# The first token block's experts chosen in two parts of four heads, the first part during the query projection

## The chip, the cores and the metric

The kernel runs on one core of a Trainium2 chip. The metric is device time in microseconds (us), the median over runs. The core has a tensor engine (PE, with its weight loads as PEld), a vector engine (DVE), an activation engine (ACT), a fourth engine (POOL), which after the start only gathers rows by index, and SP, which issues all the other transfers. Each engine works through its own instructions in order, and waits where an instruction needs another engine or a transfer.

## The reference: what is computed

A decoder layer over 1024 tokens of width 1024, in float32:

```python
h   = layer_norm(x)
mix = token_mixer(h)            # stick-breaking attention + mLSTM, gated, projected
h   = layer_norm(ALPHA * h + mix)
ffn = peer_ffn(h)               # experts
ple = sigmoid(h @ w_ple_gate) * (p @ w_ple)
h   = layer_norm(ALPHA * h + ffn + ple)
```

The experts (`peer_ffn`): for each token and each of 8 heads two query halves are scored against 128 keys each, the 16 best of each half are kept, the 16 best of their 256 sums are taken, and these give 16 of 16384 experts. So each token has 8 x 16 = 128 experts. With u and v the two tables of 16384 rows, a token's output is the sum over its experts of gate * gelu(h . u[expert]) * v[expert].

## The kernel before

**Blocks.** The tokens are cut into 8 token blocks of 128 (`tb` 0 to 7), one token on each partition. These are worked in three blocks: (0, 1), (2, 3, 4) and (5, 6, 7). Each block passes through `project`, `attention`, `recurrent`, `mlstm`, `branch`, `keys`, `choose` and `embed`; the next block's `pre` and `project` are merged into the end of the one before.

**Two ways to the experts.** Token blocks 7, 3 and 4 (`DENSE`) are done densely: `spread` turns the choice into a table of gates in DRAM (`Gd`), and `dense` then multiplies the tokens with all 16384 experts on PE, in 128 groups, at the end of the kernel. Token blocks 0, 1, 2, 5 and 6 are done by rows: for each of the 128 slots POOL gathers a 4 KB row for every token (512 KB in all, L1116), first from u and then from v, and DVE works on it with one scalar_tensor_tensor (listed under L142, a helper's line). That makes 5 x 256 = 1280 gathers. Their order is fixed: all u rows of a token block come before its v rows, and the v rows of one token block alternate with the u rows of the next, if that one's experts are known.

**Buffers.** Gathered rows go into six buffers of the tag `vr` (`K` = 6). For block 0 the same six buffers also hold, split into two halves for extra precision (`Halves`), the activations `o.h1` that `keys` and `embed` multiply: four of the six. They come free when `embed`'s last matmul with them is done.

**Query projection and choice.** `keys` projects the queries in four units; each gives two heads. For every half head, `best` finds the 16 best keys (five DVE operations on 128 x 128: L818 to L822). In block 0 the scores of the second token block are put aside (`o.hold`) and `best` is run for it later, inside `choose`. `choose` then does, for all 8 heads of a token block at once: 50 candidate sums (`cv`), the 16 best of them head by head, the candidates' expert numbers (`ci`), a match of positions to numbers (`eq`, `idf`), and the indices as integers (`vidx`); after that the gates (`gt`). The weights of block 0 are split in two on ACT and DVE before PE uses them (DVE's part is L259).

**Order.** The program is written by Python generators that yield planned microseconds. `Merge` interleaves generators by planned time. A background stream (`Experts`) is stepped whenever the planned time of the main work passes its own; one step writes a u row and a v row where both are due. In `Experts.add` a token block enters the list only when two calls have come: one from `choose` (gates ready), one from `embed` (its base sum `based` stored). The written order is a priority: a scheduler at compile time orders each engine's instructions on a modelled timeline. DVE operations of `choose` go through `cvec`, a chain of depth 20 (`CD`), those of the rows through `evec`, a chain of depth 1.

Of the kernel before, what the change touches and what calls it, by code (L numbers as in the profile page):

```python
# [73 lines left out]
FAST = {0}  # L74
FASTQ = {0}
SLOTS = 5
W = 384


# [43 lines left out]
def body(ctx: ExitStack, tc: tile.TileContext, a, out):  # L123
# [763 lines left out]
    def choose(o, tbs):  # L887
        for tb in tbs:
            j = tb - o.tbs[0]
            V, I = o.VI[j]  # L890
# [5 lines left out]
            t4 = csel("top", (P, 4, P))  # L896
            fI = t4[:, 0:2, :].rearrange("p a (h k) -> p a h k", h=NH)
            ts = t4[:, 2, :].rearrange("p (h k) -> p h k", h=NH)
            fp = t4[:, 3, :].rearrange("p (h k) -> p h k", h=NH)
            cvec.tensor_copy(fI, I)  # L900
            cvec.tensor_scalar(fI[:, 0], fI[:, 0], 128.0, None, op0=OP.mult)
            cv = csel("cv", (P, NH, NC50))
            ci = csel("ci", (P, NH, NC50))
            def sums(dst, src, of, a0, a1, b0, b1):
                na, nb = a1 - a0, b1 - b0
                d = dst[:, :, of:of + na * nb]
                l, r = src[:, 0, :, a0:a1], src[:, 1, :, b0:b1]
                if na == 1:
                    l = l.to_broadcast([P, NH, nb])
                elif nb == 1:  # L910
                    r = r.to_broadcast([P, NH, na])
                else:
                    d = d.rearrange("p h (a b) -> p h a b", b=nb)
                    l = l[:, :, :, None].to_broadcast([P, NH, na, nb])
                    r = r[:, :, None, :].to_broadcast([P, NH, na, nb])
                cvec.tensor_tensor(d, l, r, op=OP.add)

            for of, a0, a1, nb in RANKS:
# [12 lines left out]
            cvec.tensor_copy(fp, pos)  # L931
            cvec.tensor_scalar(fp, fp, STEP, None, op0=OP.mult)
            idf = T([P, NH, 16], F32, "idf", 1)
# [4 lines left out]
            cvec.tensor_tensor(ci, ci, posn[:, None, :].to_broadcast([P, NH, NC50]), op=OP.add)  # L938
            yield 2.5
            for i, (_, n) in enumerate(CLASSES):  # L940
                k = slice(4 * i, 4 * i + 4)
                step = NH if n * 4 * NH <= D else NH // 2
                for h in range(0, NH, step):
                    h = slice(h, h + step)
                    shape = [P, step, 4, n]
                    eq = c4("eq")[:, :step * 4 * n].rearrange("p (h k n) -> p h k n", h=step, k=4)
                    cvec.tensor_tensor(eq, ci[:, h, None, :n].to_broadcast(shape),
                                       fp[:, h, k, None].to_broadcast(shape), op=OP.subtract)
                    cvec.tensor_reduce(idf[:, h, k], eq, axis=AX.X, op=OP.min, apply_absolute_value=True)
                    yield 2 * (step * 4 * n + 60) * 1.05e-3  # L950
            vidx = T([P, P], U32, "vidx", 5)
            x = cvec.tensor_copy(vidx, idf.rearrange("p h k -> p (h k)"))
            gt = T([P, NH, 16], F32, "gt", 5)
            cvec.tensor_tensor(gt, ts, ts[:, :, 0:1].to_broadcast([P, NH, 16]), op=OP.subtract)
            act.loose(gt, gt, AF.Exp)
            sm = T([P, NH], F32, "sm", 1)
            cvec.tensor_reduce(sm, gt, axis=AX.X, op=OP.add)
            cvec.reciprocal(sm, sm)
            cvec.tensor_tensor(gt, gt, sm[:, :, None].to_broadcast([P, NH, 16]), op=OP.mult)
            if tb in DENSE:  # L960
                yield from spread(tb, vidx, gt)
            else:
# [137 lines left out]
    class Experts:  # L1100
        def __init__(self):
# [1 line left out]
            self.e = self.v = None  # L1103
            self.fifo = []
            self.rate = 1.0
            self.half = []

        def add(self, tb):

            self.half.append(tb)  # L1110
            if self.half.count(tb) == 2:
                self.todo.append(tb)

        def row(self, idx, s, use):
            vr = T([P, D], F32, "vr", K)
# [14 lines left out]
        def first(self, tb):  # L1130
# [146 lines left out]
```

## Time and profile before

| what | value |
|---|---|
| median of 3 runs | 3270.45 us (3263.51 to 3273.95) |
| profiled execution, own time | 3266.96 us |
| its span, first to last instruction | 3265.2 us |
| mean granted PE clock | 0.947 of full |
| busy: PE, DVE, POOL, ACT | 2928.7, 2616.4, 1571.5, 1086.9 us |
| moved by DMA | 1035.20 MB |

The own time is the span with 1.8 us around it. A busy share is a mean over stages that are limited by different things, so each stage is read by itself. Times in the rows are counted from the span's start.

### The profile page before, as it was taken

How to read it: one execution, taken by the hardware profiler on the slowest of the kernel's cores; microseconds unless marked ns; L12 is line 12 of the kernel's file. 1: busy time of each engine (PE TensorE's matmuls, PEld its weight loads, DVE VectorE, ACT ScalarE, POOL GpSimd, SP SyncE). 2: the span in 40 equal slices, each digit the busy share in tenths (PEclk: the TensorE clock that was granted, in tenths of full speed). 3: DMA queues.
4: the chain of work that ended last, by engine and by line, in shares of the span. 5: the costliest groups of instructions: out<-in, count | busy, mean ns of one | idle time of the engine just before them, and what ended most of it. 6: DMA issues, size and time to landing. Idle time of an engine off the chain costs nothing.

```text
span 3265.2 us, 39000 instructions
## 1 busy us (share of the span) xinstructions
PE 2928.7 (90%) x12201; PEld 1994.7 (61%) x12201; DVE 2616.4 (80%) x5551; ACT 1086.9 (33%) x2574; POOL 1571.5 (48%) x1313
## 2 busy tenths in 40 slices
PE   7997999969899937999898986999999999999990
PEld 7886655645464535667655554666666666666660
DVE  5635898898799998988987999977666777777788
ACT  5626335421621458656414135111111111111110
POOL 0000065667633543576765353455554555554564
PEclk9998999979999968999999998999999999999995
DMA  6444698989989978898899899999999999999997
GB/s 220 131 143 144 230 365 310 379 304 374 382 289 314 343 290 314 298 373 304 298 380 346 305 338 322 358 365 349 349 354 358 348 355 343 352 353 332 367 327 275
DMA packets 341823, 1035.20 MB, mean 317 GB/s; under 512 B 38512, under 2 KB 95216, under 8 KB 341616
## 3 DMA queue, kind: packets, MB, share of 16 engines
q0 software_dynamic: 184320, 671.17, 56.7%
q1 hardware_dynamic: 157296, 361.55, 30.7%
q8 instruction: 96, 1.57, 0.2%
q14 instruction: 111, 0.91, 0.1%
HBM read 991.17 MB, written 41.42 MB: 316 GB/s over the span
## 4 chain that ended last, share of the span: by engine, by line
PE 66%; DVE 16%; issue 7%; ACT 7%; DMA 4%; POOL 1%; SPq 0%; DVEq 0%; POOLq 0%; ACTq 0%
PE g L282 14%; PE g L1047 13%; PE z L1047 7%; PE m L286 5%; PE m L284 5%; PE m L285 5%; DVE acc L142 3%; PE g L798 3%; ACT ohB L164 2%; DVE vr L142 2%; PE g L286 2%; PE g L284 2%; PE g L285 2%; PE m L622 1%; PE m L1032 1%
## 5 line engine op out<-in xcount | busy, mean ns | idle before, releaser
L1116 POOL DMA_INDIRECT vr<-in_u_dram,vidx x640 | 782.0, 1222 | 982.4 <-DVE V L142 383.6
L1116 POOL DMA_INDIRECT vr<-in_v_dram,vidx x640 | 785.9, 1228 | 683.4 <-DVE acc L142 289.4
L142 DVE SCALAR_TENSOR_TENSOR acc<-vr,w,acc 128x1024 f32<-128x1024 f32 x640 | 818.8, 1279 | 57.1 <-DMA vr<-in_v_dram,vidx 47.1
L142 DVE SCALAR_TENSOR_TENSOR vr<-vr,h1r 128x1024 f32<-128x1024 f32 x640 | 780.3, 1219 | 64.8 <-DMA vr<-in_u_dram,vidx 51.4
L164 ACT ACTIVATE hl<-wf 128x512 fp32r<-128x512 f32 x240 | 151.2, 631 | 909.9 <-PE m L285 779.0
L1047 PE MATMUL g<-wf,y 128*128 128x512 f32 x960 | 431.3, 592 | 0.0
L259 DVE TENSOR_TENSOR hl<-wf,hl 128x512 fp32r<-128x512 f32 x240 | 167.7, 699 | 285.9 <-ACT hl L164 247.5
L284 PE MATMUL m<-h1s,hl 128*128 128x384 f32 x960 | 370.3, 386 | 0.0
L282 PE MATMUL g<-hT,wf 128*128 128x384 f32 x1024 | 343.1, 491 | 3.2 <-DVE gs L865 3.2
L286 PE MATMUL m<-h1s,hl 128*128 128x384 f32 x960 | 322.9, 336 | 0.0
L285 PE MATMUL m<-h1s,hl 128*128 128x384 f32 x960 | 322.2, 336 | 0.0
L1047 PEld LDWEIGHTS g<-wf,y 128*128 128x128 f32 x960 | 180.3, 189 | 173.0 <-issue 172.1
L282 PEld LDWEIGHTS g<-hT,wf 128*128 128x128 f32 x1024 | 193.1, 192 | 137.4 <-issue 11.0
L1047 PE MATMUL z<-wf,y 128*128 128x512 f32 x480 | 225.5, 592 | 0.0
L285 PEld LDWEIGHTS m<-h1s,hl 128*128 128x128 f32 x960 | 180.6, 188 | 28.7 <-issue 28.7
L284 PEld LDWEIGHTS m<-h1s,hl 128*128 128x128 f32 x960 | 180.6, 188 | 28.7 <-issue 28.7
L286 PEld LDWEIGHTS m<-h1s,hl 128*128 128x128 f32 x960 | 180.3, 188 | 0.0
L1001 PE MATMUL z<-ohA,ohB 128*128 128x128 f32 x768 | 134.5, 319 | 42.6 <-DVE ohB L999 17.5
L282 PE MATMUL g<-h1T,wf 128*128 128x384 f32 x512 | 172.5, 492 | 0.0
L1047 PEld LDWEIGHTS z<-wf,y 128*128 128x128 f32 x480 | 91.2, 190 | 114.8 <-issue 114.8
L1001 PEld LDWEIGHTS z<-ohA,ohB 128*128 128x128 f32 x768 | 111.6, 212 | 68.0 <-ACT ohB L164 46.1
L259 DVE TENSOR_TENSOR wf<-wf 128x1024 fp32r<-128x1024 f32 x68 | 83.1, 1222 | 69.9 <-ACT wf L164 67.1
(350 smaller groups left out, 4725.5 us busy)
## 6 DMA issues: line engine op xcount, KB each, us to landing
wf<-in_uE_dram SPq DMA_DIRECT2D x128, 512.0 KB
wf<-in_v_dram SPq DMA_DIRECT2D x128, 512.0 KB
wf<-in_wmain_dram SPq DMA_DIRECT2D x84, 512.0 KB
wf<-in_wgate_dram SPq DMA_DIRECT2D x48, 512.0 KB
wf<-in_wq_dram SPq DMA_DIRECT2D x48, 512.0 KB
Gd<-stage SPq DMA_DIRECT2D x48, 512.0 KB
gp<-Gd SPq DMA_DIRECT2D x32, 768.0 KB
wf<-in_wout_dram SPq DMA_DIRECT2D x24, 512.0 KB
```

The lines of the kernel that those rows point to most:

```text
L142: x = getattr(vec, op)(*args, **kw)
L164: x = nc.scalar.activation(o, i, f, **kw)
L259: vec.tensor_tensor(lo, src, hi, op=OP.subtract)
L282: pe.matmul(o, l[0], r[0], start=first, stop=last)
L284: pe.matmul(o, l[0], r[0], start=first, stop=False)
L285: pe.matmul(o, l[0], r[1], start=False, stop=False)
L286: pe.matmul(o, l[1], r[0], start=False, stop=last)
L622: pe.matmul(pw[:, c], sp[:, c], nident, start=False, stop=True, skip_group_check=True)
L798: pe.matmul(acc, yT[k // 4][:, k % 4, n * P:(n + 1) * P], wo[u][k // 2][:, k % 2, :], start=k == 0, stop=k == 7)
L1001: pe.matmul(pg[:, k], B[:, k], A[:, k], start=True, stop=True)
L1047: pe.matmul(acc[d][c], y[:, d * P:(d + 1) * P], wv[:, c * 512:(c + 1) * 512], start=e == 0, stop=e == P - 1)
L1116: pool.indirect_dma_start(out=vr, out_offset=None, in_=use[0], in_offset=bass.IndirectOffsetOnAxis(ap=idx[:, s:s + 1], axis=0))
```

## The change

`choose` for one token block becomes a generator `pick` that takes a list of head ranges. For token block 0 it gets two ranges, heads 0 to 3 and heads 4 to 7 (`PARTS`). The first part is merged into the third unit of the query projection (the one with number 2), behind the second unit, which delivers the last of heads 0 to 3; the second part runs where `choose` ran. After a part, `vidx` holds 64 of the 128 slots, and `Experts.known` lets the rows of these slots be written; `first` waits in planned time for the rest. For block 0 the u rows no longer wait for `embed`; the v rows still do (`stored`). All other token blocks are chosen in one range, with the same operations as before, but `pick` yields head by head (1.3 each) where `choose` yielded 2.5 for four heads, so that its planned cost is larger. In block 0 the scratch tile `eq` comes from the tag `c6` and no longer from `c4`.

```diff
+PARTS = {1: (0, 4), 3: (4, 8)}
...
+        o.pick = pick(o, o.tbs[0], PARTS.values()) if o.hold else None
+
+        def part():
+            for c in o.pick:
+                if c is None:
+                    break
+                yield c
+
         for u in range(4):
-            yield from gemm(o.q["q"][u], r1, range(4), ev_q(u), False, w)
+            g = gemm(o.q["q"][u], r1, range(4), ev_q(u), False, w)
+            yield from Merge(g, part()) if o.hold and u - 1 in PARTS else g
...
+            if o.hold and j == 0:
+                yield from o.pick
+            else:
+                yield from (c for c in pick(o, tb, [(0, NH)]) if c is not None)
+
+    def pick(o, tb, parts):
...
+        for h0, h1 in parts:
+            n = h1 - h0
+            hs = slice(h0, h1)
...
-            yield 2.0
-            pos = T([P, NH, 16], U32, "pos", 1)
-            for h in range(NH):
+            yield 0.25 * n
+            for h in range(h0, h1):
                 c = cv[:, h, :]
                 cvec.max(ts[:, h, 0:8], c)
...
-                if h % 4 == 3:
-                    yield 2.5
...
+                yield 1.3
...
-            yield 2.5
-            for i, (_, n) in enumerate(CLASSES):
+            yield 0.3 * n
+            for i, (_, m) in enumerate(CLASSES):
                 k = slice(4 * i, 4 * i + 4)
-                step = NH if n * 4 * NH <= D else NH // 2
-                for h in range(0, NH, step):
+                step = n if m * 4 * n <= D else n // 2
+                for h in range(h0, h1, step):
...
-                    eq = c4("eq")[:, :step * 4 * n].rearrange("p (h k n) -> p h k n", h=step, k=4)
...
+                    eq = (c6("eq", (P, 4 * W)) if o.hold else c4("eq"))[:, :step * 4 * m].rearrange("p (h k n) -> p h k n", h=step, k=4)
...
+            cs = slice(h0 * 16, h1 * 16)
+            x = cvec.tensor_copy(vidx[:, cs], idf[:, hs].rearrange("p h k -> p (h k)"))
+            if tb not in DENSE:
                 chosen[tb] = vidx, gt
-                cvec.gate = x if o.hold and j == 0 else None
-                ex.add(tb)
-                yield 1.0
+                ex.known(tb, h1 * 16)
+            if h1 < NH:
+                yield None
...
-            self.half = []
+            self.n, self.stored = {}, set()
+
+        def known(self, tb, n):
+
+            if tb not in self.n:
+                self.todo.append(tb)
+            self.n[tb] = n
 
         def add(self, tb):
 
-            self.half.append(tb)
-            if self.half.count(tb) == 2:
-                self.todo.append(tb)
+            self.stored.add(tb)
...
             for s in range(P):
+                while s >= self.n[tb]:
+                    yield ROW_US
...
-            if self.e is None and self.todo and len(self.ready) < 1:
+            if self.e is None and self.todo and len(self.ready) < 1 and (
+                    self.todo[0] in BLOCKS[0] or self.todo[0] in self.stored):
                 self.e = self.first(self.todo.pop(0))
-            if self.v is None and self.ready:
+            if self.v is None and self.ready and self.ready[0][0] in self.stored:
                 self.v = self.second(*self.ready.pop(0))
```

## Rows read from the trace of the kernel before

**Rows 1.** The page's chain that ended last, shares by engine.
```profile
PE 66%; DVE 16%; issue 7%; ACT 7%; DMA 4%; POOL 1%; SPq 0%; DVEq 0%; POOLq 0%; ACTq 0%
```

**Rows 2.** Windows: length; busy PE, PEld, DVE, ACT, POOL (xinstructions); clock, DMA share, GB/s.
```profile
2054.00:3184.00 1130.00, 1130.00 (x4351) 778.29 (x4349) 827.20 (x1354) 198.03 (x361) 596.09 (x476) 1.00 0.97 352
3184.00:3244.00 60.00, 0.55 (x2) 0.00 (x0) 54.89 (x46) 0.00 (x0) 40.49 (x36) 0.53 0.92 337
```

**Rows 3.** Timeline of POOL: start, length, what; idle before and its releaser.
```profile
2035.06 1.17 POOL L1116 DMA_INDIRECT vr<-in_v_dram,vidx  x1 [0.66 <-DVE top L142]
2054.20 0.94 POOL L1116 DMA_INDIRECT vr<-in_u_dram,vidx  x1 [17.97 <-DVE top L142]
```

**Rows 4.** DVE, choice of token block 5: first and last operation, rows' share (window).
```profile
2001.28 0.28 DVE L142 CAST top<-I 128x256 f32<-128x256 uint16 x1
...
2053.72 0.22 DVE L142 CAST vidx<-idf 128x128 uint32<-128x128 f32 x1
...
2001.00:2054.00 53.00, 20.36 (x16) 0.81 0.89 290
```

**Rows 5.** The chain that ended last, around the dense stage's start.
```profile
2004.95 6.19 DMA Gd<-stage
...
2011.21 12.08 DMA gp<-Gd
```

**Rows 6.** Timeline of POOL at its first gathers, 385 to 403 us.
```profile
385.91 1.09 POOL L1116 DMA_INDIRECT vr<-in_u_dram,vidx  x1 [381.68 <-DVE V L142]
...
392.27 0.94 POOL L1116 DMA_INDIRECT vr<-in_u_dram,vidx  x1 [0.30 <-issue]
402.88 0.94 POOL L1116 DMA_INDIRECT vr<-in_u_dram,vidx  x1 [9.67 <-DVE I L142]
```

**Rows 7.** DVE ends the second unit; then tile vr, 330 to 460 us, first:last start.
```profile
322.13 0.29 DVE L822 FIND_INDEX8 I<-V,sc 128x8 uint16<-128x128 f32 x1
...
L1116 POOL DMA_INDIRECT vr<-in_u_dram,vidx x33: 932/960/2252, 385.9 to 459.0; - x33
...
L286 PE MATMUL g<-wf,vr x32: 388/392/398, 342.1 to 372.2; 128*128 128x512 f32 x32
...
L142 DVE SCALAR_TENSOR_TENSOR vr<-vr,h1r x28: 1177/1222/1230, 401.4 to 458.7; 128x1024 f32<-128x1024 f32 x28
```

**Rows 8.** Windows at the query projection's end: all engines; L259 alone; L142 alone.
```profile
322.00:355.50 33.50, 32.93 (x220) 28.86 (x219) 22.52 (x76) 14.96 (x33) 0.00 (x0) 1.00 0.51 171
355.50:385.00 29.50, 29.24 (x103) 19.11 (x102) 29.40 (x132) 9.73 (x11) 0.00 (x0) 1.00 0.71 236
...
322.00:355.50 33.50, 11.11 (x10) 1.00 0.51 171
...
355.50:385.00 29.50, 20.30 (x117) 1.00 0.71 236
```

**Rows 9.** Timeline of DVE: five small sums of the choice, one after another.
```profile
371.43 0.51 DVE L142 TENSOR_TENSOR ci<-top 128x32 f32<-128x32 f32 x5
```

**Rows 10.** Timeline of POOL and DVE behind the last matmul.
```profile
3187.28 10.53 DVE L142 SCALAR_TENSOR_TENSOR acc<-vr,w,acc 128x1024 f32<-128x1024 f32 x8
3189.15 1.54 POOL L1116 DMA_INDIRECT vr<-in_v_dram,vidx  x1 [1.18 <-DVE acc L142]
3190.99 1.01 POOL L1116 DMA_INDIRECT vr<-in_v_dram,vidx  x1 [0.30 <-issue]
3192.31 1.02 POOL L1116 DMA_INDIRECT vr<-in_v_dram,vidx  x1 [0.30 <-issue]
...
3198.41 1.28 DVE L142 SCALAR_TENSOR_TENSOR acc<-vr,w,acc 128x1024 f32<-128x1024 f32 x1 [0.61 <-DMA vr<-in_v_dram,vidx]
```

**Rows 11.** DVE's waits for gathered u rows, whole run: total us, times, longest.
```profile
DVE vr L142 <- DMA vr<-in_u_dram,vidx: 51.4, 62, 2.1
```

**Rows 12.** Windows over the second block's choice and spread.
```profile
1000.00:1200.00 200.00, 167.50 (x624) 104.37 (x623) 193.21 (x566) 84.42 (x228) 101.02 (x82) 0.91 0.93 339
1200.00:1400.00 200.00, 144.30 (x689) 101.59 (x690) 182.65 (x355) 122.20 (x332) 97.87 (x78) 0.88 0.82 289
```

More of the change, by code (lines that the diff above doesn't have):

```diff
@@ L889, in choose @@
             j = tb - o.tbs[0]
-            V, I = o.VI[j]
             if o.hold and j == 1:
@@ new lines, in pick @@
+    def pick(o, tb, parts):
+        j = tb - o.tbs[0]
+        V, I = o.VI[j]
+        t4 = csel("top", (P, 4, P))
+        fI = t4[:, 0:2, :].rearrange("p a (h k) -> p a h k", h=NH)
+        ts = t4[:, 2, :].rearrange("p (h k) -> p h k", h=NH)
+        fp = t4[:, 3, :].rearrange("p (h k) -> p h k", h=NH)
+        cv = csel("cv", (P, NH, NC50))
+        ci = csel("ci", (P, NH, NC50))
+        pos = T([P, NH, 16], U32, "pos", 1)
+        idf = T([P, NH, 16], F32, "idf", 1)
+        vidx = T([P, P], U32, "vidx", 5)
+        gt = T([P, NH, 16], F32, "gt", 5)
+        for h0, h1 in parts:
+            n = h1 - h0
+            hs = slice(h0, h1)
@@ L904, in sums @@
             def sums(dst, src, of, a0, a1, b0, b1):
                 na, nb = a1 - a0, b1 - b0
-                d = dst[:, :, of:of + na * nb]
-                l, r = src[:, 0, :, a0:a1], src[:, 1, :, b0:b1]
+                d = dst[:, hs, of:of + na * nb]
+                l, r = src[:, 0, hs, a0:a1], src[:, 1, hs, b0:b1]
                 if na == 1:
-                    l = l.to_broadcast([P, NH, nb])
+                    l = l.to_broadcast([P, n, nb])
                 elif nb == 1:
-                    r = r.to_broadcast([P, NH, na])
+                    r = r.to_broadcast([P, n, na])
@@ L912, in sums @@
                 else:
                     d = d.rearrange("p h (a b) -> p h a b", b=nb)
-                    l = l[:, :, :, None].to_broadcast([P, NH, na, nb])
-                    r = r[:, :, None, :].to_broadcast([P, NH, na, nb])
+                    l = l[:, :, :, None].to_broadcast([P, n, na, nb])
+                    r = r[:, :, None, :].to_broadcast([P, n, na, nb])
                 cvec.tensor_tensor(d, l, r, op=OP.add)
+            cvec.tensor_copy(fI[:, :, hs], I[:, :, hs])
+            cvec.tensor_scalar(fI[:, 0, hs], fI[:, 0, hs], 128.0, None, op0=OP.mult)
@@ L928, in choose @@
                 cvec.max_index(pos[:, h, 8:16], ts[:, h, 8:16], c)
-                if h % 4 == 3:
-                    yield 2.5
-            cvec.tensor_copy(fp, pos)
-            cvec.tensor_scalar(fp, fp, STEP, None, op0=OP.mult)
-            idf = T([P, NH, 16], F32, "idf", 1)
+                yield 1.3
+            cvec.tensor_copy(fp[:, hs], pos[:, hs])
+            cvec.tensor_scalar(fp[:, hs], fp[:, hs], STEP, None, op0=OP.mult)
             for blocks, _ in CLASSES:
@@ L936, in choose @@
                     sums(ci, fI, to, *ab)
-            cvec.tensor_tensor(ci, ci, posn[:, None, :].to_broadcast([P, NH, NC50]), op=OP.add)
-            yield 2.5
-            for i, (_, n) in enumerate(CLASSES):
+            cvec.tensor_tensor(ci[:, hs], ci[:, hs], posn[:, None, :].to_broadcast([P, n, NC50]), op=OP.add)
+            yield 0.3 * n
+            for i, (_, m) in enumerate(CLASSES):
                 k = slice(4 * i, 4 * i + 4)
-                step = NH if n * 4 * NH <= D else NH // 2
-                for h in range(0, NH, step):
+                step = n if m * 4 * n <= D else n // 2
+                for h in range(h0, h1, step):
@@ L944, in choose @@
                     h = slice(h, h + step)
-                    shape = [P, step, 4, n]
-                    eq = c4("eq")[:, :step * 4 * n].rearrange("p (h k n) -> p h k n", h=step, k=4)
-                    cvec.tensor_tensor(eq, ci[:, h, None, :n].to_broadcast(shape),
+                    shape = [P, step, 4, m]
+                    eq = (c6("eq", (P, 4 * W)) if o.hold else c4("eq"))[:, :step * 4 * m].rearrange("p (h k n) -> p h k n", h=step, k=4)
+                    cvec.tensor_tensor(eq, ci[:, h, None, :m].to_broadcast(shape),
@@ L948, in choose @@
                                        fp[:, h, k, None].to_broadcast(shape), op=OP.subtract)
                     cvec.tensor_reduce(idf[:, h, k], eq, axis=AX.X, op=OP.min, apply_absolute_value=True)
[L950 to L962, printed above, removed]
-                chosen[tb] = vidx, gt
-                cvec.gate = x if o.hold and j == 0 else None
-                ex.add(tb)
-                yield 1.0
+                    yield 2 * (step * 4 * m + 60) * 1.05e-3
@@ new lines, in pick @@
+            cs = slice(h0 * 16, h1 * 16)
+            x = cvec.tensor_copy(vidx[:, cs], idf[:, hs].rearrange("p h k -> p (h k)"))
+            if tb not in DENSE:
+                chosen[tb] = vidx, gt
+                ex.known(tb, h1 * 16)
+            if h1 < NH:
+                yield None
+        cvec.tensor_tensor(gt, ts, ts[:, :, 0:1].to_broadcast([P, NH, 16]), op=OP.subtract)
+        act.loose(gt, gt, AF.Exp)
+        sm = T([P, NH], F32, "sm", 1)
+        cvec.tensor_reduce(sm, gt, axis=AX.X, op=OP.add)
@@ L968, in spread @@
+        cvec.reciprocal(sm, sm)
+        cvec.tensor_tensor(gt, gt, sm[:, :, None].to_broadcast([P, NH, 16]), op=OP.mult)
+        if tb in DENSE:
+            yield from spread(tb, vidx, gt)
+        else:
+            cvec.gate = x if o.hold and j == 0 else None
+            yield 1.0
     def spread(tb, vidx, gt):
```

8 lines of the change are left out of this document (removed).

## The prediction

> **What bounds the kernel now.** I read the page's chain that ended last first. PE has two thirds of it [rows 1], but a share doesn't say what a gather that comes earlier is worth, so I went to the windows from the end backwards. From 2054 to 3184 us, the dense stage, PE is busy all of the time, the DMA engines 0.97 of it, and POOL issues 476 gathers, one per 2.374 us (1130 / 476). Then PE is done, and 36 gathers are left, which take 60 us, 1.667 us each [rows 2]; after them come 21 us of layer norms. 476 + 36 = 512 are the gathers of token blocks 5 and 6. So the end hangs on two moments: **t5**, at which the first of these 512 can go, and **D**, at which the dense stage ends. If t5 comes x later and D comes y later, (y - x) / 2.374 more rows are done by D and each saves 1.667: the end moves by 0.702 x + 0.298 y.
>
> What sets t5? The timeline of POOL shows the last gather of token block 2 at 2035.06, then 18 us in which POOL has nothing to gather, and the first of token block 5 at 2054.20 [rows 3]. That one waits for `vidx` of block 5, cast at 2053.72; its choice began at 2001.28 [rows 4]. So the row stream has already run dry there. Gathers that start earlier in block 0 don't end the kernel earlier by themselves: they lengthen this dry stretch. They help only as far as DVE, which multiplies the rows, is then free for block 5's choice: within it DVE spends 20.36 us on 16 rows of token block 2 [rows 4]. D is set elsewhere: by the end of `spread`, then a store of 6.19 us and a load of 12.08 us of the gate table [rows 5].
>
> **What the change moves.** Now the first gather goes at 385.91, and six can be in flight before a buffer comes back at 402.88 [rows 6]. The scores of heads 0 to 3 have been searched by 322.4 (322.13 + 0.29) [rows 7].
>
> The cost of the first part: the choice takes 20.30 us of DVE under L142 in 355.5 to 385 [rows 8]. Some 1 us of that are the gates, which stay whole; half of the rest is 9.65 us. Counting in the diff, 24 sums for `ci`, 7 for `cv` and 6 copies, scalings and additions are issued twice with half the heads, and `eq` with its reduction 8 times each where it was 6: 41 more instructions. The maxima and their indices go head by head already and don't multiply. Five small sums take 0.51 us [rows 9], so I take 0.08 us of fixed cost each: 3.3 us, half of it in the first part, which is then 11.3 us. DVE was idle for 33.5 - 22.52 = 11.0 us in 322 to 355.5 [rows 8]: it fits, with nothing to spare. With three weight splits of 1.11 us (11.11 / 10 [rows 8]) ahead of parts of it, the first 64 indices stand at 322.4 + 11.3 + 3.3 = 337 us. Bounds: 334 without the splits, 355.5 if the best-key searches of the last two units go first. I take 338, because the part is written before those searches.
>
> How many rows get ahead: four of the six row buffers hold the activations until `embed`'s last matmul with them, at 372.2 [rows 7]. So for 34 us two buffers circulate. Behind the last matmul the row of the first of the eight rows in a run frees a buffer for the gather at 3189.15; two gathers later, at 3192.31, goes the row that DVE then has to wait for, until 3198.41 [rows 10]: 6.1 us from issue to data. With 1.22 us on DVE and 0.3 us to hand over, a buffer is back after 7.6 us, so a row goes every 3.8 us: 9 rows by 372.2. Then six buffers, at the steady 2.374 us: 6 rows by 385.9. **15 rows ahead**; at least 8 (two, then six), at most 20 (48 us at 2.374).
>
> The Trainium skill, DMA: Bandwidth & Descriptors, "Anatomy of one DMA", gives about 2.0 us plus the bytes over 436 GB/s for a transfer of this kind, an estimate of 3.2 us for 512 KB. The row shows 6.1 us, beside other gathers. By the page a buffer would be back after 4.7 us, some 20 rows would get ahead, and the end would come 0.9 us earlier than in the sum below, which goes by the row.
>
> The Trainium skill, SBUF — State Buffer, "SBUF: two separate sides", speaks against the change: POOL cannot write a gather's descriptors while DVE runs certain two-port operations, and DVE will be full just where the early gathers go. The first 33 gathers went beside a full DVE, and POOL's spans for them are 0.96 us at the median and 2.25 us at the longest [rows 7]: the rule doesn't show in most of them. Were all as long as the longest, a buffer would be back after 8.9 us, one row fewer would get ahead, and the end would come 0.9 us later than in the sum.
>
> **The sum.** Each row done early takes 20.36 / 16 = 1.27 us of DVE out of block 5's choice [rows 4]; 15 rows take out 19.1 us. Bounds: nothing, if the choice is held by something else, and 20.36, since more rows than 16 don't lie in it. The early stage costs something: the 3.3 us of extra instructions, and whatever PE loses where DVE's weight splits come late. PE is busy 32.93 of 33.5 and 29.24 of 29.5 us there [rows 8], so its loss would not be won back. I take 3 us for both together, from 0 (DVE's own idle time hides it) to 10 (three weight splits of block 0's last ten lost behind rows). The store and load of the gate table, 18.3 us, lie beside gathers; with fewer of these I take 2 us off, from 0 to 4. The other moved or added pieces I cost at nothing: no transfer is added, and `h1r`'s one load, on SP, lies beside DMA engines that are busy 0.51 of the time [rows 8] (a load late by all of its 6 us would cost two rows); `eq` in another tag is the same work, if a tile of that tag is free (if not, the second part is late, and with it rows that have a buffer only after 372.2).
>
> So x = 3 - 19.1 = -16.1 and y = 3 - 2 = +1, and the end moves by 0.702 * -16.1 + 0.298 * 1 = -11.0 us. From the profiled execution's own 3266.96 that is 3256; the median of its runs is 3.5 us higher, 3270.45, so for a median I say **3257**.
>
> **The rivals.**
>
> *Fewer rows get round.* If the scheduler doesn't pass the two free buffers round before the other four come back, 8 rows get ahead: x = 3 - 10.2 = -7.2, y = 2, the end -4.5 us: 3262. Or the choice of block 5 doesn't move with the rows, since its order on DVE was set on a modelled timeline, and the dry 18 us [rows 3] simply grow: x = y = 3, 3270. For it: the gain must pass through one choice of 53 us in which DVE also waits for the gate table. Against: DVE's rows in that stretch are real work in its order.
>
> *Slower: early rows hold up DVE.* DVE works in order, and with two buffers a row's multiplication follows its gather closely. If DVE stands for the whole 6.1 us once for each of the 4.5 pairs, that is 27 us, the weight splits queue behind it, PE waits for the splits, and everything later moves by 27 + 3 = 30 us: the end by 0.702 * (30 - 19.1) + 0.298 * 28 = +16 us, 3283. It decides from a loss of 24 us on (24 - 13.9 = 10 us). Against: in the whole run DVE waited for u rows 62 times, 2.1 us at the longest [rows 11], and 4.5 such waits are 9.5 us. For: those rows had six buffers.
>
> *The finer steps in all token blocks.* The planned cost of a choice grows by 5.3 (10.4 for 5.0, 2.4 for 2.5). In the second block three choices and two `spread` follow one another; this places them up to 16 planned us later against `embed` and `project`. PE is idle there for 32.5 + 55.7 us while DVE is busy 193 and 183 of 200 [rows 12]. Either sign: 16 us later for all, with the gain of 11, is 3272; 16 us of PE's idle time won is 3241.
>
> **How the numbers follow.** Chances: my sum 0.42, fewer rows or a choice that stays 0.30, DVE held up 0.15, the finer steps 0.13 (0.04 faster, 0.03 same, 0.06 slower). About 0.3%, 10 us, is what a measurement of this kernel can tell from no change. Faster by more: 0.46; within: 0.33; slower: 0.21. The sum's own range, with its costs at their bounds, is 3252 to 3264. The range takes in the fewer rows (3262, 3270) and the held-up DVE but for its worst, and on the other side part of the finer steps: 3243 to 3282.
>
> **What the profile would show.** The first gather of u at about 338, and some 9 gathers by 372, in pairs. In 322 to 372 PE still busy for over 97%. The last v gather of token block 2 about 35 us earlier against the choice of block 5, fewer than 6 rows inside that choice, and its `vidx` near 2038. The stretch behind the last matmul shortened from 36 gathers to about 29. I am wrong if the first gather comes after 360, if DVE waits for gathers in 338 to 372 for more than 10 us, if rows still stand between the operations of block 5's choice, or if `spread` of the second block ends at another time.

## The result, and the profile after

The changed kernel takes **3296.61 us** (median of 4 runs, 3292.57 to 3299.71), the kernel before 3270.8 in runs beside it: a ratio of 1.0078, 95% interval 1.0063 to 1.0093. It is 26 us slower. I had said 3257, with 3243 to 3282 as the range, and had given slower 0.21. The likeliest case and the range were both wrong.

The profiled execution spans 3290.6 us (before: 3265.2). The early rows came as forecast. Timeline of POOL, changed kernel (start, length, what, idle before and its releaser):

```profile
339.39 1.69 POOL L1146 DMA_INDIRECT vr<-in_u_dram,vidx  x1 [335.16 <-DVE sc L822]
341.38 1.13 POOL L1146 DMA_INDIRECT vr<-in_u_dram,vidx  x1 [0.30 <-issue]
346.31 1.68 POOL L1146 DMA_INDIRECT vr<-in_u_dram,vidx  x1 [3.80 <-DVE vr L144]
...
367.12 0.94 POOL L1146 DMA_INDIRECT vr<-in_u_dram,vidx  x1 [3.98 <-DVE I L824]
...
387.02 0.94 POOL L1146 DMA_INDIRECT vr<-in_u_dram,vidx  x1 [1.09 <-ACT gs L166]
388.27 0.94 POOL L1146 DMA_INDIRECT vr<-in_u_dram,vidx  x1 [0.30 <-issue]
```

The first gather goes at 339.4, not at 385.9 [rows 6], eight have gone by 372, and 14 before the time at which the kernel before issued its first. But the projections around them (the rest of the queries and the base sum up to 372 us, then the second block's), which had kept PE busy [rows 8], now have holes. Windows of the kernel before and of the changed kernel (columns as in [rows 2]), then the changed kernel's PE waits in 320 to 440 us:

```profile
322.00:372.00 50.00, 49.16 (x281) 40.20 (x280) 38.98 (x179) 19.85 (x39) 0.00 (x0) 1.00 0.55 185
372.00:427.00 55.00, 52.00 (x140) 25.49 (x139) 54.78 (x270) 9.84 (x16) 19.51 (x17) 0.97 0.87 297
```

```profile
322.00:372.00 50.00, 39.13 (x225) 32.77 (x225) 40.87 (x174) 17.10 (x36) 10.92 (x8) 0.92 0.61 211
372.00:427.00 55.00, 40.23 (x132) 23.88 (x130) 49.38 (x213) 7.32 (x10) 18.81 (x17) 0.90 0.89 316
```

```profile
PE g L284 <- ACT stored L166: 12.0, 1, 12.0
PE g L287 <- DVE wf L261: 6.1, 2, 4.8
PE g L288 <- DVE wf L261: 3.6, 1, 3.6
PE m L284 <- DMA wiff<-in_wif_dram: 2.7, 1, 2.7
```

10 and 12 us of PE's busy time are lost there. Its mean granted clock is 0.92 and 0.90 instead of 1.00 and 0.97; what this adds to the lag was not separated. PE waits for weight splits on DVE (`wf`), for the gate weights of the second block (`wiff`), and for 12 us behind `stored`, which on ScalarE stands behind `fl`, and that behind `ifg`, the gate sum on DVE. The first store of the second block's keys (`kTd`), kernel before and changed kernel (ns of one, lowest/median/highest, then first and last start):

```profile
L523 SPq DMA_DIRECT2D kTd<-stored x4: 327/402/2112, 401.7 to 404.8; - x4
```

```profile
L525 SPq DMA_DIRECT2D kTd<-stored x4: 327/392/448, 426.9 to 428.3; - x4
...
L1082 SPq DMA_DIRECT2D gp<-Gd x32: 359/514/6263, 2052.6 to 3063.6; - x32
```

That is a lag of 25 us. It grows to 41 us by the first load of the gate table (`gp`, 2052.6 instead of 2011.2 [rows 5]) and is 36 at the end of the dense stage (D, 3220.8 instead of 3184.5). The lead of the rows shrinks with it: by 459 us the changed kernel has issued 39 gathers and the kernel before 33.

The end of the kernel gained, and more than forecast. Changed kernel, POOL, then DVE, around the choice of token block 5, to set beside [rows 3, 4]:

```profile
2009.06 0.94 POOL L1146 DMA_INDIRECT vr<-in_v_dram,vidx  x1 [1.77 <-DVE ohB L1025]
2070.02 0.93 POOL L1146 DMA_INDIRECT vr<-in_u_dram,vidx  x1 [60.02 <-DVE top L144]
```

```profile
2043.76 0.29 DVE L144 CAST top<-I 128x256 f32<-128x256 uint16 x1
...
L144 DVE CAST vidx<-idf x1: 224/224/224, 2069.5 to 2069.5; 128x128 uint32<-128x128 f32 x1
```

No row of token block 2 is left in that choice: 25.8 us instead of 52.4. But it starts 42.5 us later, so t5 is 15.8 us later, and D 36.2. The prediction's own formula gives 0.702 * 15.8 + 0.298 * 36.2 = 22 us for these two; the span grew by 25.4.

Something else is new, on ScalarE. Its instructions by line (count, then busy us and mean ns), and a piece of its timeline in the second block's attention:

```profile
L166 ACT ACT_TABLE_LOAD x52 | 66.7, 1283 | 1.8 <-DVE cqk L546 0.8
L162 ACT ACT_TABLE_LOAD x19 | 24.4, 1283 | 1.0 <-PEq L1299 0.7
```

```profile
481.15 1.28 ACT L166 ACT_TABLE_LOAD   x1
482.45 0.52 ACT L166 ACTIVATE asp<-asp 128x384 f32<-128x384 f32 x1
482.99 1.28 ACT L166 ACT_TABLE_LOAD   x1
484.28 0.52 ACT L166 ACTIVATE asp<-asp 128x384 f32<-128x384 f32 x1
```

Loads of the function table now stand between the activations of that attention, 49 of them in 428 to 700 us: 88 loads in the kernel instead of 39. Where it starts is seen at the Exp of the first choice, changed kernel and then the kernel before:

```profile
386.87 1.28 ACT L162 ACT_TABLE_LOAD   x1
391.77 0.31 ACT L173 ACTIVATE gt<-gt 128x128 f32<-128x128 f32 x1 [3.62 <-DVE gt L144]
392.10 1.28 ACT L175 ACT_TABLE_LOAD   x1
```

```profile
372.10 1.28 ACT L171 ACT_TABLE_LOAD   x1
373.40 0.31 ACT L171 ACTIVATE gt<-gt 128x128 f32<-128x128 f32 x1
373.73 1.28 ACT L173 ACT_TABLE_LOAD   x1
...
375.63 1.28 ACT L160 ACT_TABLE_LOAD   x1
```

The helper `loose` runs a lone Exp and loads the old table again behind it. In the kernel before this restoring load (L173) comes ahead of the switch to the attention's table (L160). In the changed one the choice ends later, the switch (L162) passes it, and the restoring load (L175) throws the attention's table out again.

### The profile page after: what moved, and what is told of

The parts are those of the page before. It is cut to its first block, busy times and chain, and to the rows that moved or that the text cites. A ratio compares the mean times of both kernels' runs of the same rounds, so it can differ in the third digit from the quotient of the medians.

```text
span 3290.6 us, 39074 instructions
## 1 busy us (share of the span) xinstructions
PE 2945.0 (89%) x12201; PEld 2001.2 (61%) x12201; DVE 2619.5 (80%) x5592; ACT 1147.9 (35%) x2623; POOL 1591.6 (48%) x1313
## 4 chain that ended last, share of the span: by engine, by line
PE 63%; DVE 16%; issue 8%; ACT 7%; DMA 4%; POOL 2%; SPq 0%; DVEq 0%; POOLq 0%; ACTq 0%
PE g L1073 13%; PE g L284 12%; PE z L1073 7%; PE m L288 5%; PE m L286 5%; PE m L287 5%; PE g L800 3%; DVE acc L144 3%; POOL vr L1146 2%; DMA vr<-in_v_dram,vidx 2%; ACT ohB L166 2%; PE g L287 2%; PE g L288 2%; DMA vr<-in_u_dram,vidx 2%; PE g L286 2%
## 5 line engine op out<-in xcount | busy, mean ns | idle before, releaser
L1146 POOL DMA_INDIRECT vr<-in_v_dram,vidx x640 | 808.9, 1264 | 644.0 <-DVE acc L144 282.8
L144 DVE SCALAR_TENSOR_TENSOR acc<-vr,w,acc 128x1024 f32<-128x1024 f32 x640 | 829.0, 1295 | 64.0 <-DMA vr<-in_v_dram,vidx 56.0
L284 PEld LDWEIGHTS g<-hT,wf 128*128 128x128 f32 x1024 | 193.3, 192 | 137.4 <-issue 11.3
L284 PE MATMUL g<-wf,hT 128*128 128x512 f32 x288 | 129.1, 604 | 12.9 <-ACT stored L166 12.9
```

Source lines behind the costliest of these rows:

```text
L144: x = getattr(vec, op)(*args, **kw)
L284: pe.matmul(o, l[0], r[0], start=first, stop=last)
L1146: pool.indirect_dma_start(out=vr, out_offset=None, in_=use[0], in_offset=bass.IndirectOffsetOnAxis(ap=idx[:, s:s + 1], axis=0))
```

## The experiments

Three marks tell where a kernel stands: the first `kTd` store (the projection's lag), the first `gp` load (the main program's lag at the dense stage) and the first u gather of token block 5 (t5). Each mark is from one profiled execution. Ratios are to the kernel before, in runs on the same chip.

| kernel | median us | ratio, 95% | kTd | gp | t5 |
|---|---|---|---|---|---|
| before | 3266 to 3271 | | 401.7 | 2011.2 | 2054.2 |
| changed | 3296.61 | 1.0063 to 1.0093 | 426.9 | 2052.6 | 2070.0 |
| e3_one_part | 3270.73 | 0.9997 to 1.0016 | 401.4 | 2013.9 | 2052.5 |
| e4_old_steps | 3297.26 | 1.0069 to 1.0102 | 427.6 | 2058.0 | 2075.1 |
| e1_tables | 3444.63 | 1.0523 to 1.0558 | 426.9 | 2199.4 | 2219.0 |
| e5_tables_rows_late | 3353.94 | 1.0245 to 1.0281 | 425.9 | 2110.0 | 2128.9 |
| e6_one_table | 3284.57 | 1.0032 to 1.0066 | 429.9 | 2045.9 | 2063.3 |
| e7_cast_once | 3271.79 | 1.0005 to 1.0026 | 408.8 | 2013.4 | 2055.3 |
| e9_no_products | 3283.57 | 1.0032 to 1.0065 | 421.9 | 2033.3 | 2056.3 |
| e10_no_gathers | 3280.0 | 1.0018 to 1.0039 | 407.1 | 2032.7 | 2052.7 |
| e11_gate_early | 3280.87 | 1.0028 to 1.0050 | 408.3 | 2033.0 | 2058.2 |
| e12_gate_early_no_products | 3266.53 | 0.9981 to 1.0002 | 405.7 | 2016.0 | 2041.6 |
| e13_19_rows_fewer | 3257.68 | 0.9957 to 0.9982 | 402.9 | 2015.9 | 2035.6 |
| e14_40_rows_fewer | 3252.11 | 0.9929 to 0.9956 | 401.9 | 2010.5 | 2029.8 |
| e15_pool_products | 3290.59 | 1.0057 to 1.0084 | 401.7 | 2031.3 | 2064.9 |
| e16_before_pool | 3324.58 | 1.0152 to 1.0182 | 404.1 | 2044.4 | 2134.1 |

The marks of e12 are those of its second run (3265.31 us), since its first profiled execution lay 26 us above its median, with `gp` at 2043.0. So a mark can be off by that much in a single execution; what made this one late is not known.

**e3_one_part: all of the diff but the two parts.**

```
-PARTS = {1: (0, 4), 3: (4, 8)}
+PARTS = {3: (0, 8)}
```

> The changed kernel with one part of eight heads for token block 0 too, chosen behind the projection as before. What is left of the change are the finer planned steps, the other tag of the scratch tile, and that the rows of token block 0 no longer wait for its base sum. ACT has 39 table loads in it, as before. Theory A: all of the loss belongs to the two parts, so this is 3270 within 6 us. Theory D (the finer steps in all token blocks cost): 3280 or more, with the lag growing behind 1000 us, in the second block.

The ratio is 1.0007. The finer steps, the other buffer for `eq` and the rows' new conditions cost nothing that shows. The loss belongs to the two parts.

**e4_old_steps: the two parts, with the old coarse steps in all other choices.**

```
-                yield 1.3
+                if len(parts) > 1:
+                    yield 1.3
+                elif h % 4 == 3:
+                    yield 2.5
...
-            yield 0.3 * n
+            yield 0.3 * n if len(parts) > 1 else 2.5
```

> The changed kernel with the coarse planned steps of before in all token blocks but the first. 88 table loads, as in the changed kernel. Theory A: 3296 within 6 us. Theory D (the finer steps cost): 3280 or less.

It is as slow as the changed kernel. With e3 this rules the finer steps out.

**e1_tables and e5_tables_rows_late: the restoring load tied to its place, for every lone activation.** e5 is also meant to make the first block's rows wait for the stored base sum.

```
-                order(nc.scalar.preload_act_table_set(self.table), x)
+                back = nc.scalar.preload_act_table_set(self.table)
+                order(back, x)
+                self.used += [x, back]
```

```
-                    self.todo[0] in BLOCKS[0] or self.todo[0] in self.stored):
+                    self.todo[0] in self.stored):
```

> The changed kernel, in which the restoring table load behind a lone Exp of the gates must now come before the next table switch; nothing else differs. The changed kernel has 49 more table loads on ACT (1.283 us each), nearly all between 428 and 700 us, where its lag behind the kernel before grows from 25 to 42 us. Theory A (the misplaced restoring load causes this second part): ACT's table loads fall from 88 to about 36, the lag stays 25 us at the first store of K (426 us) and is still 25 us at the end of the first attention, and the time falls by about 17 us, to 3280. Theory B (the second part comes from more rows beside the attention, and ACT's loads are hidden): the loads fall all the same, the lag grows to 42 us again, and the time stays at 3296.

> As the run with the restoring load in its place, and in addition the rows of token block 0 wait for its base sum again, as in the kernel before; the choice in two parts stays where the change put it. Theory A (the first part of the lag, 25 us by 426 us, comes from rows that follow their gathers too closely on DVE): the stretch from 320 to 426 us is as fast as before within 5 us, no wait of DVE for gathers before 372, the dry stretch of POOL before token block 5 is back near 18 us, the time 3265 to 3275. Theory C (the 11 us of the choice's first part on a nearly full DVE cause it): PE still loses some 20 us there, the early rows' gain at token block 5 is gone, and the time is 3285 to 3295.

Both misfired. The loads fell to 36, and the attention of the second block ran without them, but every later switch of the table now had to wait for a lone activation that itself waits for rows. Waits of ScalarE and PE in e1_tables, whole run (us, times, longest):

```profile
ACT w L173 <- DVE vr L144: 124.9, 4, 115.4
PE z L599 <- ACT art L166: 128.0, 7, 124.8
```

One Gelu held ScalarE for 115 us. And e5 did not make the rows late: its first gather went at 341.2, so it says nothing about them. Each got a narrower successor.

**e6_one_table: the same order for the first choice's Exp alone.**

```
-        def loose(self, o, i, f):
+        def loose(self, o, i, f, tight=False):
...
-                order(nc.scalar.preload_act_table_set(self.table), x)
+                back = nc.scalar.preload_act_table_set(self.table)
+                order(back, x)
+                if tight:
+                    self.used += [x, back]
...
-        act.loose(gt, gt, AF.Exp)
+        act.loose(gt, gt, AF.Exp, o.hold and j == 0)
```

> The changed kernel with one more order: the restoring load behind the first choice's Exp must come before the next switch of the table, and this for that one Exp only. Theory A (19 row products that stand on VectorE ahead of block 1's gate sum cost the first 25 us of the lag; the restoring load in the wrong place costs the other 17): table loads back from 88 to 39, the first K store of block 1 still near 427, the lag from block 1's attention on 25 us instead of 37 to 42, the last choice's indices near 2053, and the end at 3276 where that choice stays free of rows, up to 3290 where rows come back into it. Rival B (the second part of the lag is the early rows' traffic beside the attention): loads fall, the lag stays near 40, 3293 to 3300.

39 loads again, and 11 us back: 15.1 us behind the kernel before in its own runs instead of 25.8, with intervals that just touch. The `gp` lag falls by 6.7 us, to 34.7; I had expected 17. So the table is a part of the loss, and a smaller one than I thought. The rest of the lag's growth, from 28 us at the `kTd` store to 35, has another cause.

**e7_cast_once: two parts, but all indices cast behind the second, so no early row.**

```
-            x = cvec.tensor_copy(vidx[:, cs], idf[:, hs].rearrange("p h k -> p (h k)"))
...
+        x = cvec.tensor_copy(vidx, idf.rearrange("p h k -> p (h k)"))
+        if tb not in DENSE:
+            chosen[tb] = vidx, gt
+            ex.known(tb, P)
```

> The changed kernel with its choice in two parts, but with the indices of all eight heads cast once, behind the second part, so that no row can be fetched before it; no change of table orders beside it. Theory A: the first gather near 386 to 395, no row product or a few ahead of the gate sum, first K store 401 to 407, the end within 6 us of the kernel before (3265 to 3277). Rival C (the lag is the choice's own first part, 11 us of VectorE work inside the projection): first K store at 412 or later and the end at 3280 or more, rows or none.

Within 0.26% of the kernel before, the first gather at 385.4, the first store 7.1 us late (a little outside the range of theory A), `gp` late by 2.2 us, one table load too many instead of 49. The choice's own first part in the projection, which I had priced at 11.3 us of DVE in 11.0 of idle time, is not what costs at the end: the early rows are. They bring two things, products on DVE and traffic on the DMA engines.

**e9_no_products and e10_no_gathers: e6 without the one or the other, for the first 19 rows.** In e9 (`skip` is 19) their weights are zero; in e10 (`fake` is 19) h1 is multiplied by itself in place of the row.

```
-                self.row(vidx, s, (a["u"], lambda vr, s=s: evec.scalar_tensor_tensor(
+                self.row(vidx, s, (a["u"], lambda vr, s=s: s < skip or evec.scalar_tensor_tensor(
```

```
+            fake = 19 if tb == BLOCKS[0][0] else 0
...
+                if s < fake:
+                    vr = T([P, D], F32, "vr", K)
+                    y = evec.scalar_tensor_tensor(vr, h, 1.0, h, op0=OP.mult, op1=OP.mult, accum_out=w[:, s:s + 1])
+                    order(y, self.x, mybir.DependencyClass.Sync)
...
```

> e6_one_table with the first 19 products of the first token block left out (their gathers stay, their weights are set to zero). Theory A (VectorE's time for the products, 19 x 1.31 us, and its waits for them, 14 us): first K store 400 to 408 and the end at 3265 to 3280. Rival B (the gathers themselves, on the DMA engines and GpSimd, beside the key projection and the halves of h1): first K store stays near 420 to 427, though the products are gone, and the end at or above that of e6_one_table.

> e6_one_table with the first 19 gathers of the first token block left out and their products kept: each multiplies the block's own h1 by itself, behind the same half of the indices. VectorE has the same work, the DMA engines and GpSimd have none of the early rows. Theory A (VectorE's products ahead of the gate sum): first K store at 418 to 430 as with the gathers (429.9). Theory B (the gathers' traffic makes the loads of the projection late, the gate weights' above all): first K store at 400 to 412, and the end below 3276.

By the first store each speaks for the traffic: without products it is still 20 us late, without gathers only 5. But the kernel without gathers is 25 us late at the attention's first `qz`, the one without products still 20. In time neither gets much back: 14.1 and 11.5 us behind the kernel before, where e6 is 15.1. What holds PE in e9, 10.2 us, is the matmul with the gate weights. The issue of their two loads on SP's queue and DVE's zeroing of their tile, in the kernel before, the changed kernel and e9:

```profile
L495 SPq DMA_DIRECT2D wiff<-in_wif_dram x2: 556/608/660, 376.8 to 377.4; - x2
L493 DVE MEMSET wiff<- x1: 298/298/298, 376.5 to 376.5; 128x288 f32 x1
```

```profile
L497 SPq DMA_DIRECT2D wiff<-in_wif_dram x2: 556/4316/8077, 393.6 to 394.2; - x2
L495 DVE MEMSET wiff<- x1: 298/298/298, 393.2 to 393.2; 128x288 f32 x1
```

```profile
L500 SPq DMA_DIRECT2D wiff<-in_wif_dram x2: 555/4504/8454, 385.2 to 386.4; - x2
L498 DVE MEMSET wiff<- x1: 298/298/298, 384.5 to 384.5; 128x288 f32 x1
```

With the early gathers the second load sits 8 us in its issue instead of 0.66, and PE starts on the weights at 409.6 (changed) or 412.6 (e9) instead of 386.7. In e10, without the first 19 gathers, the second load's issue takes 3.97 us and PE starts at 397.0. In e9 the trace puts PE's wait down to DVE's `ci`; but DVE's only work for that tile, its zeroing, was done at 384.8, so the load is what is left, and the next pair of runs bears it out. The loads follow DVE's zeroing within 0.7 us, and that itself comes 17 us later in the changed kernel, behind 11 of the 19 products: the products delay these weights too. The gate sum thus stands behind two late things at once: 19 products ahead of it on DVE, and weights that land late. In the changed kernel the products come last (the gate matmuls end at 414.9, the sum starts at 423.9, and DVE doesn't wait for PE); in e9 the weights do. To take one away leaves the other.

**e11_gate_early and e12_gate_early_no_products: e6 with these weights fetched at the kernel's start; then the 19 products left out too.**

```
-        wiff = c2("wiff", (P, 8, 64))
+        wiff = o.wiff or gate_weights(c2("wiff", (P, 8, 64)))
...
+                blks[1].wiff = gate_weights(T([P, 8, 36], F32, "wif1"))
```

> e6_one_table with block 1's gate weights (two loads of 16 KB) fetched at the start of the kernel into a tile of their own, all early rows kept. Theory B (TensorE waits for these weights, whose issue stood 8 us on the queue and landed 7 us later): first K store at 405 to 418, the end at 3268 to 3279. Theory A (products ahead of the gate sum alone): first K store stays at 424 to 430, the end near 3284.

> e11_gate_early with the first 19 products left out as well (their gathers stay, their weights are set to zero). If the products on VectorE and the late gate weights are the whole of the lag: first K store at 400 to 408, the end at 3255 to 3270. If another load of the projection is late in the same way (the main weights of 512 KB, which landed after 10 us instead of 5): first K store at 412 or later, TensorE's waits in 380 to 420 are for these weights, and the end is 3272 to 3284.

> e12_gate_early_no_products once more, for a profile that stands near its median (its first profiled execution took 3292 us, its median is 3266.5). If the 9 us between it and e13_19_rows_fewer are a lag of the main program: the first store of the dense stage comes 8 to 15 us later than in the kernel before and the last choice is empty of rows all the same. If they are rows that still hold the last choice: the main program is within 4 us of the kernel before, and the choice takes 35 us or more.

With the weights early, the first store stands at 408.3, but the lag comes back behind it: 15 us at the attention's first `qz`, 22 at `gp`. With the products gone as well it is 4 us at the store, 2 at `qz` and 5 at `gp`, and the time is that of the kernel before. So the lag is taken apart in this order: at `gp` 41.4 us, without the table reloads 34.7, without the late weights 21.8, without the products 4.8; in time, against the kernel before in each one's runs, 25.8, 15.1, 12.4 and -2.0 us. Of the last two steps only the second is clear of noise in time, and the shares hang on the order: with the products out first (e6, e9, e12) that step brings 1 us and the weights then bring 16. Nor does e11 only undo a delay: the gate sum goes at 376.4, 22 us earlier than in the kernel before and ahead of 11 of the 19 products, so that the products now come behind it. The kernel before with its weights fetched early was not run, so a gain of that edit by itself may be in these figures. e11's end lies 2 us above the range of theory B. The second run, 3265.31 with a ratio of 0.9981 to 1.0005, matches neither of its two cases: the main program is 4.8 us late and the last choice takes 31 us.

**e13_19_rows_fewer and e14_40_rows_fewer: the kernel before, with 19 or 40 rows of its first token block not done at all.** This is the head start for nothing, and a little more than that, since the rows' work is gone from the whole kernel.

> The kernel before, with the first 19 rows of its first token block left out altogether, gather and product (their weights are set to zero). This is the change's head start with nothing paid for it. The prediction's gain: 15 rows or more of relief empty the last choice of its rows, its indices come 16 to 20 us earlier (2034 to 2038), and the end falls by 0.702 of that, to 3255 to 3258. Rival F (the row work gets the time back elsewhere, and the last choice is rarely held up by rows): the last choice stays between 40 and 52 us or the main program ahead of it comes no earlier, and the end is 3264 to 3270.

> The same with 40 rows left out. The prediction's gain is then at its cap of 20.4 us in the last choice, and what the other 20 rows give back elsewhere on VectorE comes on top: 3240 to 3256. Rival F: under 0.3% again, 3260 to 3270.

```
-            for s in range(P):
+            skip = 19 if tb == BLOCKS[0][0] else 0
+            if skip:
+                vec.memset(w[:, :skip], 0.0)
+            for s in range(skip, P):
```

The gain is there: 3257.68, ratio 0.997, and 3252.11 with 40 rows left out. In e13 the choice of token block 5 runs without rows, and t5 comes 18.6 us earlier than in [rows 3]. POOL and DVE:

```profile
2035.60 0.94 POOL L1116 DMA_INDIRECT vr<-in_u_dram,vidx  x1 [56.02 <-DVE pos L142]
```

```profile
2007.19 0.29 DVE L142 CAST top<-I 128x256 f32<-128x256 uint16 x1
...
L142 DVE CAST vidx<-idf x1: 239/239/239, 2034.8 to 2034.8; 128x128 uint32<-128x128 f32 x1
```

**e15_pool_products and e16_before_pool: can the products go elsewhere?** e11 with the 19 products on GpSimd, summed on ScalarE; and the kernel before with 40 so done.

```
+    def beside(vr, h, w):
+        pool.tensor_tensor(vr, vr, h, op=OP.mult)
+        act.activation(vr, vr, AF.Copy, accum_out=w)
```

> e11_gate_early with the first 19 products moved off VectorE: GpSimd multiplies the row by h1, ScalarE sums it. All the work of the change is done. Theory A (the last 14 us of the loss are VectorE's time for these products): first K store 402 to 408, block 1's first attention 441 to 446, and with the rows' head start the last choice free of rows: 3256 to 3266, faster than the kernel before. Rival G (the two-part choice and the early gathers cost the main program about 9 us beside the products, the difference between e12_gate_early_no_products and e13_19_rows_fewer; and GpSimd's products hold up the gathers behind them): 3266 to 3280.

> The kernel before, choice in one part, with only the products of the first 40 rows of its first token block moved to GpSimd and ScalarE. If VectorE's time is what the rows are short of, as e14_40_rows_fewer says (16 us for 40 rows that cost nothing), it is 3252 to 3264. If GpSimd, which issues the gathers behind the products, is then what the rows wait for: 3266 or more.

No. GpSimd needs twice DVE's time for a product, and ScalarE, which the attention needs, stands behind it. e15_pool_products, POOL's products over the whole run and ScalarE's largest wait in 330 to 520 us (total, times, longest):

```profile
L1134 POOL TENSOR_TENSOR vr<-vr,h1r 128x1024 f32<-128x1024 f32 x19 | 46.0, 2436 | 12.3 <-DMA vr<-in_u_dram,vidx 12.2
```

```profile
ACT vr L166 <- POOL vr L1134: 29.2, 12, 5.2
```

Its first `kTd` store is back at 401.7, but the fourth goes at 430, and `gp` is 20 us late. At 3290.59 it lies above both of its cases. e16, with 40 products on GpSimd, takes 3324.58, 57 us more than the kernel before, and its rows of token block 2 run on until the first u gather at 2134.1.

## Why the prediction was wrong

**What bounds the kernel: right, with a price that is off.** With each profiled execution's own t5 and D the formula gives 22 us for the changed kernel (its span grew by 25), 0.702 * 9.1 + 0.298 * 29.3 = 15 for e6 (18), 7 for e11 (13), -9 for the second run of e12 (-3.5) and 0.702 * -18.6 + 0.298 * 1.1 = -13 for e13 (-10). The two moments order the kernels rightly, but the formula is 3 to 6 us too low each time. A part of that is a misreading: the 60 us behind the dense stage hold the landing and the product of the last gather, which are paid once. The 36 gathers themselves go out in 51.9 us (the last at 3236.4), 1.44 us each, which makes it 0.607 x + 0.393 y; 1 to 4 us are still missing, and their cause is open.

**When the early rows go: right.** 339 for 338, eight rows by 372 for nine, 14 ahead for 15.

**The gain: right in size where it costs nothing.** In the changed kernel the main program's own lag gave the rows time too. The head start by itself shows in e13: `vidx` at 2034.8, where I had said 2038, and -9.4 us where the sum said -11.0. The choice of token block 5 shrank by 24.8 us, a little more than the cap of 20.36 that I had set. With the early gathers paid for and only the products left out (e12, second run), t5 still comes 12.6 us earlier, but no gain clear of noise is left.

**The cost of the early stage: the step that failed.** I took 3 us, at most 10, for "the 3.3 us of extra instructions, and whatever PE loses where DVE's weight splits come late". The main program came 25 us late at the first store and 36 at D, where I had put y at +1. The term left out the early rows' own work in the place where they go, their products above all. I counted each product at 1.27 us as relief in token block 5's choice and at nothing where they go now. DVE's groups from 322 us to the gate sum (at 398.9 before, at 423.9 now), the first of the changed kernel and the first of the kernel before:

```profile
L144 DVE SCALAR_TENSOR_TENSOR vr<-vr,h1r 128x1024 f32<-128x1024 f32 x19 | 23.2, 1221 | 14.1 <-DMA vr<-in_u_dram,vidx 14.0
```

```profile
L259 DVE TENSOR_TENSOR wf<-wf 128x1024 fp32r<-128x1024 f32 x14 | 17.1, 1219 | 7.7 <-ACT wf L164 7.7
```

19 products with their read-backs are 24.9 us, and DVE's waits for their gathers 14.1; the kernel before has neither there, and some 10 us of idle time to set against 39. That is 29 us by this account, 25 as measured at the gate sum. e9 and e10 bound what this proves: with the 19 products gone the gate sum is still at 419.4, held by the gate weights; with their gathers gone it is at 404.7; and yet either kernel is 20 to 25 us late at the attention's first `qz`. So the products or the gathers alone are each enough for most of that lag, and the two together do not add up. The 11 us of idle time that I had seen ahead of the choice I had already given to its first part, and e7 shows that this held to within 7 us at the first store and 2 at `gp`; for the rows nothing was left. With 25 us more in x and in y my sum would have read -11 + 25 = +14, and its sign would have been right. Of the signs that I named, two speak against me: PE is busy for 78% of 322 to 372, not for over 97, and the second block's `spread` moved (its first store goes at 1165.0 instead of 1122.8).

**Two terms that the sum did not have.** The loads of the gate weights, 16 KB each, are issued 17 us later, behind DVE's late zeroing, and then the second sits 8 us in its issue beside the early gathers, so that PE starts on them 23 us late. I had costed the transfers at nothing because none is added; but those of 19 rows were moved into the projection, ahead of these loads. And the table order on ScalarE, 11 us: a load without a fixed place among others fell behind a switch that it should precede.

**The rivals.** The slower one named the right place and a time (3283) that lacks 14 us. Its mechanism was only half of it: DVE waits for gathers 8.9 us in 338 to 372 and 14.0 by the gate sum, not 27, and it too left out the products themselves. The finer steps did nothing (e3, e4), and rows that would not get round were not the trouble.

**Open.** How the loss divides between the products and the late weights is known only in the orders given above. e12 and e13 differ by 8 us: with gathers early and products left out, t5 is 6 us later than with the rows gone altogether, 2.7 of it at the start of the last choice and 3.6 within it. Which remaining piece makes these was not separated.

## What to carry to other kernels

Work that is moved earlier must be paid where it lands: count the moved instructions' own time, their waits and their transfers in the new stretch, as relief is counted in the old one. On an engine that is full in both places the move gains only if the old place is nearer to the path than the new one; here a microsecond of lag early in the main program came back as up to one at the end, while the relief went through a single choice. If a helper reloads state without a fixed place in the order, look at the count of those reloads after any change of timing.

## What the runs showed of the hardware

A load of ScalarE's function table takes 1283 ns, each of the 88, and the next activation starts about 1.30 us after the load's start (481.15 to 482.45 in the changed kernel). The Trainium skill, ScalarE activation tables: per-element evaluation and per-set limits, "What a function is on this engine", gives the same 1283 ns between functions of two sets and none within one; the trace agrees with the first. 49 more loads are 63 us of ScalarE, of which some 11 reached the end.

A load of 16 KB isn't cheap because it is small. Beside the early gathers its issue on SP's queue took 8.1 us (the DMA engines busy throughout, 414 GB/s in 393 to 402.5), in e10 without them 3.97 us, in the kernel before 0.66. That the engines are busy doesn't tell these apart: in the kernel before they were so too (341 GB/s in 374 to 380).

A product of a 128x1024 row with its sum takes 1.22 us on DVE (changed kernel); the product alone takes 2.44 us on GpSimd (e15).
